# A one-layer HGRN2/gMLP trunk on one core: where the query-key sums, the neighbours' keys, the gate unit's roots and the second group's squares stand in the order of their engines

## Chip, cores and metric

The kernel runs on one core of a Trainium2 chip. The metric is the device time of one execution in microseconds, lower is better. The engines are PE (matrix products), DVE (vector), ACT (scalar functions), POOL (GpSimd) and SP, which issues nearly all the DMAs. PEld is the loading of weights into PE.

## The reference

One layer works on 2048 tokens of 1024 channels, with a context of 256 tokens ahead of it. Cut to what bears on the change:

```python
h = modulate(rmsnorm(x, norm_mix[l]), sh1, sc1)
p = h @ w_in[l]                                   # one projection for both head groups
# group A, 4 heads: gated linear recurrence in both directions
logf, k = log_sigmoid(f), sigmoid(-f)             # per direction
scores = einsum('bhtk,bhsk,bhtsk->bhts', qc, kc, decay)
o = o_inter + einsum('bhts,bhsv->bhtv', scores, vc)
# group B, 4 heads: gMLP gate over chunks of 128 positions
u, v = gelu(u), layernorm(gelu(v))
z = einsum('hpq,bnqhc->bnphc', w_s, v) + b_s
x = x + g1 * (concat(o_hg, u * z) @ w_out[l])
x = x + g2 * conv_ffn(modulate(rmsnorm(x, norm_ffn[l]), sh2, sc2), ...)
return rmsnorm(x, norm_final)
```

## The kernel before

**Stages.** The tokens are worked on in two halves of 1024. For each half the projection runs bank by bank: a bank is 128 columns of w_in times 512 tokens (or the 256 of the context), and it takes three products for each of the eight blocks of 128 channels, since each fp32 operand is split into a high part that is a rounded float (`xh`, `whi`) and a rest (`xl`, `wlo`). `run_banks` writes these products; between them `slot()` lets background work write its next piece. Then follow the output projection, the up-projection with the convolution, the down-projection and the last norm. The changed lines all belong to the stage with the projection, which ends before 960 us of the span.

**The order of the work.** The code is written in one order, and a planner then sets the order in which each engine gets its instructions: it goes by its own reckoning of when the inputs of an instruction are ready, and takes the one that is written first among those that are. `pin` ties an instruction behind the one that is written just before it on the same engine. It orders only these two: an unpinned instruction that is written later may still be put ahead of both. `manual_schedule` keeps the head of the kernel in written order altogether. Each engine works off its own list in order, so an instruction that waits holds up all that stand behind it.

**x's groups.** `x_start` handles the first 1024 tokens in two groups of four tiles of 128 tokens, `xg` and `xs`. For a group `x_square` (L239, ACT) gives the sums of squares, `rstd` (L126 and L128, POOL) the roots, `x_scale` (L245, DVE) multiplies the tiles by them, and `x_first` transposes them on PE and writes `xh` and `xl` (L250, L252, L253) in four steps of two channel blocks each. The squares of the second group are written between steps of the first, and its scaling behind the fourth of them. The weights of a bank are split by `split_w`: a cast on ACT (`whi`, L133) and a subtraction on DVE (`wlo`, L134).

**A head.** `hg` runs eight times, for four heads in each half. It first adds the keys of both directions (L794, DVE), multiplies by the queries (L795), and splits the product into `kh` (L798, a cast on ACT) and `kl` (L800, DVE), whose column sums PE makes with a matrix of ones: these are the query-key sums, the diagonal of the scores. Two more multiplies give `Q` for both directions (L799 and L801). Then the neighbours' products follow (L815, split in L822 into `knl`), and a loop over the levels B = 1, 2, 4, ... 64: PE makes the scores of a level from row 0 of the keys, and DVE masks them in (L846). Then `level_update` multiplies Q (L514), `level_keys` makes the next level's keys in two rows (multiplies in L591, copies on ACT in L594), and `next_tot` the next totals (L521, pinned already). In `level_keys` the loop writes row 0, then row 1. At B = 1 both multiplies are DVE's, and read the gates themselves (`K<-K,F`); these are the neighbours' keys. At higher levels row 1 is POOL's. The result of row 0 overwrites the tile that L822 reads; row 1 lies beside it in the same tile.

**The gate unit.** `sgu` runs eight times too. `ln` takes means and variances (L704, L705), `rstd` the roots on POOL, DVE normalises (L709), PE mixes the positions, DVE adds the bias (L717), and `both` multiplies by gelu(u) on POOL (L685) and stores the result.

Of the kernel before, what the change touches and what calls it, by code (L numbers as in the profile page):

```python
# [9 lines left out]
F32 = mybir.dt.float32  # L10
# [4 lines left out]
ALU = mybir.AluOpType  # L15
# [34 lines left out]
def view(t, off, dims):  # L50

    return bass.AP(t.tensor, t.offset + off, [list(t.ap[0])] + [list(d) for d in dims])
# [32 lines left out]
def tile_trunk(ctx, tc, x, c, cx, c_ctx, w_ada, b_ada, norm_mix, norm_ffn, w_in, hg_norm, sgu_g, sgu_b,  # L85
               w_sp, b_sp, w_out, w_up, conv_w, conv_b, w_down, norm_final, masks, out):
    nc = tc.nc
    V, S, G, T = nc.vector, nc.scalar, nc.gpsimd, Tensor(nc.tensor)
    ld = nc.sync.dma_start
    st = nc.sync.dma_start  # L90
    pin = tc.keep_in_program_order
# [14 lines left out]
    mhalf = cst.tile([P, 8], F32, name="mhalf")  # L106
# [16 lines left out]
    def rstd(pool, ss, n, scale, bias=EPS, keep=lambda i: i, out=None):  # L123

        r = pool.tile([P, 8], F32, tag="rs", name="rs")
        keep(G.tensor_scalar(out=r[:, :n], in0=ss, scalar1=scale, scalar2=bias, op0=ALU.mult, op1=ALU.add))  # L126
        r2 = pool.tile([P, 8], F32, tag="rs2", name="rs2") if out is None else out
        G.tensor_tensor(out=r2[:, :n], in0=r[:, :n], in1=mhalf[:, :n], op=ALU.pow)  # L128
        return r2

    def split(hi, lo, raw, eng=None, keep=lambda i: i):
# [59 lines left out]
    with es1:  # L191
        ps = es1.enter_context(tc.tile_pool(name="ps1", bufs=1, space=PSUM, reuse_waits="tile"))
        p1 = es1.enter_context(tc.tile_pool(name="p1", bufs=1, reuse_waits="tile"))
        pm = es1.enter_context(tc.tile_pool(name="pm", bufs=1, reuse_waits="tile"))
# [38 lines left out]
        def x_sums():  # L233
            return pm.tile([P, 8], F32, tag="xss", name="xss", bufs=2)

        def x_square(xs, ss, i0=0, keep=pin):
            for i, xt in enumerate(xs):
                jk = pm.tile([P, D], BF16, tag="acc", name="xjk")
                keep(S.activation(jk, xt, AF.Square, accum_out=ss[:, i0 + i:i0 + i + 1]))  # L239

        def x_scale(xs, ss, keep=pin):

            r = rstd(pm, ss[:, :len(xs)], len(xs), 1.0 / D, keep=keep)
            for i, xt in enumerate(xs):
                keep(V.tensor_scalar(out=xt, in0=xt, scalar1=r[:, i:i + 1], scalar2=None, op0=ALU.mult))  # L245
# [94 lines left out]
        with tc.manual_schedule():  # L340
# [29 lines left out]
            for k in range(NK):  # L370
                for i in range(2):
                    o = (k % 2) * 256 + i * P
# [43 lines left out]
        def x_start():  # L416
            xk = [pk.tile([P, 2, D], F32, tag="K", name="xk", bufs=2, align_bytes=AL) for i in range(2)]
            xs = [xk[i // 2][:, i % 2, :] for i in range(4)]
            ss, ss2 = ss0, x_sums()
            for q in range(2):  # L420
                x_square(xg[2 * q + 1:2 * q + 3], ss, 2 * q + 1)
                for i in range(2 * q, 2 * q + 2):
                    pin(ld(xs[i], x_rows[4 + i]))
                if q:
                    x_scale(xg, ss)
                yield 2.0
            for i, w in enumerate(x_first(0, xg)):
                if i in (1, 2):
                    x_square(xs[2 * i - 2:2 * i], ss2, 2 * i - 2)
                if i == 3:  # L430
                    x_scale(xs, ss2)
                yield w
            done.add("x0a")
            yield 3.0
            yield from x_first(4, xs)
# [139 lines left out]
        def level_keys(K, B, tot, K2=None):  # L575

            W, nb = TH, TH // B
            K2 = K2 if K2 is not None else pk.tile([P, 2, W], F32, tag="K", name="K2", bufs=2, align_bytes=AL)
            if B == P // 2:
                n = W // (2 * B)  # L580
                src = [[2 * B, n], [B, 2], [1, B]]
                t = view(tot, nb + 1, [[2, n], [-(nb + 1), 2], [0, B]])
                V.tensor_mul(view(K2, 0, [[2 * B, n], [W + B, 2], [1, B]]), view(K, 0, src), t)
                S.copy(view(K2, W, [[2 * B, n], [B - W, 2], [1, B]]), view(K, W, src))
                return K2
            n = W // (4 * B)
            for row, (o, step, t0, ts) in enumerate(((0, 3 * B, nb + 1, 1 - nb), (B, B, 0, nb + 3))):
                src = [[4 * B, n], [step, 2], [1, B]]
                e = G if row and B > 1 else V
                keep = pin if B == 1 else lambda i: i  # L590
                e.tensor_mul(view(K2, row * W + o, src), view(K, o, src), view(tot, t0, [[4, n], [ts, 2], [0, B]]))  # L591
                o2, step2 = (B, B) if row == 0 else (0, 3 * B)
                src = [[4 * B, n], [step2, 2], [1, B]]
                keep(S.copy(view(K2, row * W + o2, src), view(K, W + o2, src)))  # L594
            return K2
# [59 lines left out]
        for h in range(NH):  # L655
            F, K, vt = sets[h % 2]
# [21 lines left out]
        def sgu(hh, h):  # L678

            z, u = {}, {}  # L680

            def both(n0):
                if n0 in z and n0 in u:
                    zt = z.pop(n0)
                    G.tensor_mul(zt, zt, u.pop(n0))  # L685
                    st(oT_d[hh][:, 4 + h, n0:n0 + 512], zt)

            def su(n0, n, pj):
                u[n0] = pm.tile([P, 512], F32, tag="gu", name="gu", bufs=2)
                S.activation(u[n0], pj, AF.Gelu)  # L690
                both(n0)

            def sv(n0, n, pj):
                gv = pm.tile([P, 512], F32, tag="vv", name="gv", bufs=2)
                S.activation(gv, pj, AF.Gelu)

                def ln():
                    pt = bank("mi")
                    for i in range(4):
                        T.transpose(pt[:, i * P:(i + 1) * P], gv[:, i * P:(i + 1) * P], ident)  # L700
                    bs = pm.tile([P, 4, 6], F32, tag="bs", name="bs", bufs=2)
                    mv = pm.tile([P, 4, 2], F32, tag="mv", name="mv", bufs=2)
                    for i in range(4):
                        V.bn_stats(out=bs[:, i, :], in_=pt[:, i * P:(i + 1) * P])  # L704
                        V.bn_aggr(out=mv[:, i, :], in_=bs[:, i, :])  # L705
                    r = rstd(pm, mv[:, :, 1], 4, 1.0)
                    nt = pm.tile([P, 512], F32, tag="nt", name="nt", bufs=2)
                    for i in range(4):
                        V.tensor_scalar(out=nt[:, i * P:(i + 1) * P], in0=pt[:, i * P:(i + 1) * P],  # L709
                                        scalar1=mv[:, i, 0:1], scalar2=r[:, i:i + 1], op0=ALU.subtract, op1=ALU.mult)  # L710

                    def mix():
                        pz = bank("mi")
                        for i in range(4):
                            T.matmul(pz[:, i * P:(i + 1) * P], nt[:, i * P:(i + 1) * P], wsT[:, h, :],
                                     start=True, stop=True)
                        V.scalar_tensor_tensor(out=nt.rearrange("p (c q) -> p c q", q=P),  # L717
                                               in0=pz.rearrange("p (c q) -> p c q", q=P), scalar=sgg[:, h:h + 1],
                                               in1=view(rh, h * P, [[0, 4], [1, P]]), op0=ALU.mult, op1=ALU.add)
                        z[n0] = nt  # L720
                        both(n0)
                    hg_q.later(mix, 7.0)
                hg_q.later(ln, 4.6)
            return su, sv

# [65 lines left out]
        def hg(hh, h, F, K, qs, vt, sgt):  # L791
            Q = ph.tile([P, 2, TH], F32, tag="Q", name="Q", align_bytes=AL)
            kd = Q[:, 0, :]
            V.tensor_add(kd, K[:, 0, :], K[:, 1, :])  # L794
            V.tensor_mul(kd, kd, qs)  # L795
            kh = ph.tile([P, TH], F32R, tag="S", name="kh")
            kl = ph.tile([P, TH], F32R, tag="T1", name="kl")
            S.copy(kh, kd)  # L798
            V.tensor_mul(Q[:, 1, :], qs, F[:, 1, :])  # L799
            V.tensor_sub(kl, kd, kh.bitcast(F32))  # L800
            V.tensor_mul(Q[:, 0, :], qs, F[:, 0, :])  # L801
            yield 6.5
            pbs = [bank("sc") for g in range(2)]
# [9 lines left out]
            K2 = pk.tile([P, 2, TH], F32, tag="K", name="K2", bufs=2, align_bytes=AL)  # L813
# [10 lines left out]
            tot = F  # L824
            for l, B in enumerate(LV):
# [5 lines left out]
                for g in range(0, NCH, 4):  # L831
# [3 lines left out]
                    for i in range(4) if B > 1 else ():  # L835
                        off = (g + i) * P
                        o = pb[:, i * P:(i + 1) * P]
                        if B < 4:
                            o = view(pb, i * P, [[B, 2], [2 * B, P // (2 * B)], [1, B]])
# [9 lines left out]
                K, K2 = level_keys(K, B, tot, K2), None  # L849
                tot = next_tot(tot, TH, B)  # L850
# [4 lines left out]
            for d in range(2):  # L855
                for g in range(0, TH, 512):
                    pt = bank("mi")
                    for i in range(4):
                        o = g + i * P
# [29 lines left out]
            for g in range(0, NCH, 4):  # L889
                po = bank("mi")  # L890
                for i in range(4):
                    ch = g + i
                    sl = slice(ch * P, (ch + 1) * P)
                    o = po[:, i * P:(i + 1) * P]
# [265 lines left out]
        i = len(seq) - 4  # L1160
# [130 lines left out]
    with tc.tile_pool(name="po", bufs=1, reuse_waits="tile") as po:  # L1291
# [58 lines left out]
        xs = []  # L1350
        for t, (hh, g) in enumerate(tiles):
# [12 lines left out]
            o = ops.pop(t)  # L1364
# [16 lines left out]
            if g % 2:  # L1381
# [8 lines left out]
                xs = []  # L1390
# [7 lines left out]
    B = [[xah[:, i] if i < NR else None, xal[:, i] if i < NR - 1 else None] for i in range(7)]  # L1398
# [186 lines left out]
    for n, (u, i) in enumerate(prods):  # L1585
# [30 lines left out]
        if n == NP - 8:  # L1616
            ts = [c_tile().rearrange("p a b -> p (a b)").bitcast(F32) for i in range(2)]
# [20 lines left out]
    V = Kept(nc.vector, pin)  # L1638
# [247 lines left out]
```

## Time and profile before

| | us |
|---|---|
| median of 3 runs | 2433.7 (2433.53 to 2437.77) |
| the profiled execution, its own time | 2434.03 |
| its span in the trace | 2432.2 |

The trace is of one execution. A group of instructions is named by the line that issued it, its engine, and the tiles that it writes and reads (`kl<-Q,kh`); where a helper issues, the line is the helper's, so all matmuls have L66. Rows of the timeline give the start in the span, the duration, engine, line, operation, tiles and shapes, and in brackets how long the engine stood idle before it and what ended that wait. A row `PE sc L66 <- DVE kl L800: 1.1, 2, 0.8` in the view of waits says that PE waited for DVE's L800 for 1.1 us in total, in 2 waits, the longest of 0.8 us. In the view of windows PEclk is the clock granted to PE as a share of its full one.

### The profile page before, as it was taken

Reading aid. Unit: us, or ns where it says so; the run is one execution under the profiler, and the core shown is the slowest. Engines: PE = TensorE matmul, PEld = TensorE weight load, DVE = VectorE, ACT = ScalarE, POOL = GpSimd, SP = SyncE. Lnnn points to the kernel's source line nnn. Section 1 sums busy time; section 2 is a strip of 40 time slices with the busy share of each in tenths; the row PEclk is TensorE's granted clock in tenths of the full one; section 3 lists DMA queues with packets and bytes.
Section 4 is the critical chain, followed back from the end, with each engine's and each line's share of the span. In section 5 each row is a group of like instructions: output and inputs, shape, how many; then the busy total and the mean of one; then the engine's idle time right before and its main releaser. Section 6 shows DMA issues by size and latency. Waiting matters only on the chain.

```text
span 2432.2 us, 32291 instructions
## 1 busy us (share of the span) xinstructions
PE 2400.6 (99%) x11711; PEld 1994.5 (82%) x11711; DVE 1658.0 (68%) x2253; ACT 1044.1 (43%) x1802; POOL 865.0 (36%) x787
## 2 busy tenths in 40 slices
PE   8999999999999999999999999999999999999998
PEld 5887888888888888888788888888888888888887
DVE  5757796765786785565596666639766673676876
ACT  3654344434344443454454444434445443332243
POOL 0021110110121122000688778787888870000002
PEclk9999999999999999999999999999999999999999
DMA  8365545463355234678922222563222239834745
GB/s 303 118 201 168 155 141 175 136 221 112 114 195 173 87 105 152 215 215 262 292 85 90 91 81 91 186 230 96 86 94 84 86 108 387 284 118 148 229 152 199
DMA packets 304046, 393.28 MB, mean 162 GB/s; under 512 B 32634, under 2 KB 215682, under 8 KB 300814
## 3 DMA queue, kind: packets, MB, share of 16 engines
q1 hardware_dynamic: 300596, 390.46, 48.6%
q8 instruction: 92, 1.51, 0.3%
q10 hardware_dynamic: 3289, 0.76, 0.1%
q14 instruction: 69, 0.56, 0.1%
HBM read 283.60 MB, written 107.55 MB: 161 GB/s over the span
## 4 chain that ended last, share of the span: by engine, by line
PE 49%; issue 2%; POOL 1%; DMA 1%; DVE 0%; ACT 0%; SPq 0%; POOLq 0%; ACTq 0%; DVEq 0%
PE ux L66 19%; PE dn L66 16%; PE uz L66 14%; DMA raw<-in_w_up_dram 1%; POOL rr L1746 0%; DMA yf<-yd 0%; POOL Al L134 0%; DMA xn<-cv 0%; POOL ra L1745 0%; POOL ra L1743 0%; DVE fl L134 0%; PE ux L70 0%; ACT jk L1734 0%; ACT yst L133 0%; POOL raw L1260 0%
## 5 line engine op out<-in xcount | busy, mean ns | idle before, releaser
L1451 DVE SCALAR_TENSOR_TENSOR dn<-gp,taps,dn 128x1024 f32<-128x1024 f32 x352 | 447.9, 1283 | 97.4 <-ACT dn L1448 93.0
L66 PE MATMUL dn<-thl,mhl 128*128 128x512 f32 x1680 | 381.0, 389 | 0.0
L66 PEld LDWEIGHTS dn<-thl,mhl 128*128 128x128 f32 x1680 | 315.2, 188 | 65.6 <-issue 0.2
L134 POOL TENSOR_TENSOR Al<-raw,Ah 128x512 fp32r<-128x512 f32 x264 | 341.1, 1308 | 69.0 <-ACT Ah L133 41.1
L66 PE MATMUL pj<-xh,whi 128*128 128x512 f32 x896 | 362.4, 405 | 0.3 <-ACT whi L133 0.3
L66 PE MATMUL pj<-xh,wlo 128*128 128x512 f32 x896 | 351.0, 392 | 0.8 <-DVE wlo L134 0.8
L66 PE MATMUL pj<-xl,whi 128*128 128x512 f32 x896 | 351.7, 392 | 0.0
L133 ACT CAST Ah<-raw 128x512 fp32r<-128x512 f32 x264 | 163.0, 620 | 243.9 <-PE ux L66 125.6
L66 PE MATMUL ux<-xah,Ah 128*128 128x512 f32 x528 | 205.9, 390 | 0.5 <-ACT keep L1515 0.3
L66 PEld LDWEIGHTS pj<-xh,wlo 128*128 128x128 f32 x896 | 168.3, 188 | 36.8 <-DVE wlo L134 1.2
L66 PEld LDWEIGHTS pj<-xh,whi 128*128 128x128 f32 x896 | 168.6, 188 | 34.3 <-issue 3.5
L66 PEld LDWEIGHTS pj<-xl,whi 128*128 128x128 f32 x896 | 168.9, 189 | 30.0 <-DVE xl L253 0.2
L66 PE MATMUL dn<-wo,o 128*128 128x512 f32 x768 | 182.4, 394 | 0.0
L66 PE MATMUL uz<-yf,Ah 128*128 128x512 f32 x704 | 174.0, 389 | 0.0
L591 POOL TENSOR_TENSOR K<-K,tot 128x512 f32<-128x512 f32 x40 | 60.5, 1513 | 300.7 <-DVE tot L521 107.8
L66 PEld LDWEIGHTS dn<-wo,o 128*128 128x128 f32 x768 | 142.1, 188 | 29.1
L66 PE MATMUL ux<-yf,Ah 128*128 128x512 f32 x528 | 155.4, 389 | 0.0
L66 PEld LDWEIGHTS uz<-yf,Ah 128*128 128x128 f32 x704 | 132.1, 188 | 27.4
L66 PE MATMUL ux<-xah,Al 128*128 128x512 f32 x528 | 141.8, 390 | 1.6 <-POOL Al L134 1.6
L66 PE MATMUL ux<-xal,Ah 128*128 128x512 f32 x352 | 137.0, 389 | 0.0
L134 DVE TENSOR_TENSOR wlo<-raw,whi 128x1024 fp32r<-128x1024 f32 x68 | 84.6, 1244 | 71.3 <-ACT whi L133 68.8
L1743 POOL TENSOR_SCALAR ra<-ss 128x1 f32<-128x1 f32 x8 | 3.2, 396 | 359.5 <-ACT jk L1734 359.5
(342 smaller groups left out, 4454.3 us busy)
## 6 DMA issues: line engine op xcount, KB each, us to landing
raw<-in_w_up_dram SPq DMA_DIRECT2D x88, 512.0 KB, 3.6
mr<-m SPq DMA_DIRECT2D x85, 512.0 KB, 5.7
raw<-in_w_in_dram SPq DMA_DIRECT2D x68, 512.0 KB, 4.0
sT<-wd SPq DMA_DIRECT2D x88, 256.0 KB, 5.0
raw<-in_w_ada_dram SPq DMA_DIRECT2D x32, 512.0 KB, 4.3
yf<-yd SPq DMA_DIRECT2D x14, 1024.0 KB, 9.9
m<-cv SPq DMA_DIRECT2D x22, 544.0 KB, 2.7
raw<-in_w_down_dram SPq DMA_DIRECT2D x22, 512.0 KB, 3.7
```

Source lines behind the costliest of these rows:

```text
L66: return self.engine.matmul(out, lhsT, rhs, **kw)
L133: keep(S.copy(hi, raw))
L134: (eng or G).tensor_sub(lo, raw, hi.bitcast(F32))
L591: e.tensor_mul(view(K2, row * W + o, src), view(K, o, src), view(tot, t0, [[4, n], [ts, 2], [0, B]]))
L1451: V.scalar_tensor_tensor(out=cr, in0=gt[:, t // 3:t // 3 + RH, t % 3:t % 3 + GW], scalar=taps[:, t * NF + f:t * NF + f + 1], in1=cr, op0=A ...
L1743: G.tensor_scalar(out=a, in0=ss, scalar1=plus, scalar2=None, op0=ALU.add)
```

## The change

Five things are done. Nothing is added to or taken from what is computed.

- The root in `rstd` (L128) goes through `keep`, as the sum ahead of it (L126) does already, and the gate unit passes `pin` for it.
- The squares of x's second group are written one step of `x_first` later: behind the third and the fourth step in place of the second and the third. Its scaling stays behind the fourth.
- In `level_keys` both multiplies at B = 1 are pinned (at higher levels `keep` does nothing).
- The gate unit's last product on POOL (L685) is pinned.
- In `hg` the add, the multiply by the queries and the subtraction of `kl` are pinned (L794, L795, L800).

```diff
@@ -125,7 +125,7 @@
         r = pool.tile([P, 8], F32, tag="rs", name="rs")
         keep(G.tensor_scalar(out=r[:, :n], in0=ss, scalar1=scale, scalar2=bias, op0=ALU.mult, op1=ALU.add))
         r2 = pool.tile([P, 8], F32, tag="rs2", name="rs2") if out is None else out
-        G.tensor_tensor(out=r2[:, :n], in0=r[:, :n], in1=mhalf[:, :n], op=ALU.pow)
+        keep(G.tensor_tensor(out=r2[:, :n], in0=r[:, :n], in1=mhalf[:, :n], op=ALU.pow))
         return r2
@@ -425,8 +425,8 @@
             for i, w in enumerate(x_first(0, xg)):
-                if i in (1, 2):
-                    x_square(xs[2 * i - 2:2 * i], ss2, 2 * i - 2)
+                if i in (2, 3):
+                    x_square(xs[2 * i - 4:2 * i - 2], ss2, 2 * i - 4)
                 if i == 3:
                     x_scale(xs, ss2)
                 yield w
@@ -588,7 +588,7 @@
                 e = G if row and B > 1 else V
                 keep = pin if B == 1 else lambda i: i
-                e.tensor_mul(view(K2, row * W + o, src), view(K, o, src), view(tot, t0, [[4, n], [ts, 2], [0, B]]))
+                keep(e.tensor_mul(view(K2, row * W + o, src), view(K, o, src), view(tot, t0, [[4, n], [ts, 2], [0, B]])))
@@ -682,7 +682,7 @@
                     zt = z.pop(n0)
-                    G.tensor_mul(zt, zt, u.pop(n0))
+                    pin(G.tensor_mul(zt, zt, u.pop(n0)))
                     st(oT_d[hh][:, 4 + h, n0:n0 + 512], zt)
@@ -703,7 +703,7 @@
-                    r = rstd(pm, mv[:, :, 1], 4, 1.0)
+                    r = rstd(pm, mv[:, :, 1], 4, 1.0, keep=pin)
@@ -791,13 +791,13 @@
             kd = Q[:, 0, :]
-            V.tensor_add(kd, K[:, 0, :], K[:, 1, :])
-            V.tensor_mul(kd, kd, qs)
+            pin(V.tensor_add(kd, K[:, 0, :], K[:, 1, :]))
+            pin(V.tensor_mul(kd, kd, qs))
             kh = ph.tile([P, TH], F32R, tag="S", name="kh")
             kl = ph.tile([P, TH], F32R, tag="T1", name="kl")
             S.copy(kh, kd)
             V.tensor_mul(Q[:, 1, :], qs, F[:, 1, :])
-            V.tensor_sub(kl, kd, kh.bitcast(F32))
+            pin(V.tensor_sub(kl, kd, kh.bitcast(F32)))
             V.tensor_mul(Q[:, 0, :], qs, F[:, 0, :])
```

## Prediction

> **What bounds the kernel now.** First the page, then the waits of PE alone, then the order of time around the places that the change touches.
>
> ```profile
> span 2432.2 us, 32291 instructions
> PE 2400.6 (99%) x11711; PEld 1994.5 (82%) x11711; DVE 1658.0 (68%) x2253; ACT 1044.1 (43%) x1802; POOL 865.0 (36%) x787
> ```
>
> PE sets the time: it is idle for 2432.2 - 2400.6 = 31.6 us of the span. The edits add and remove no instruction, they only reorder DVE, ACT and POOL. They can therefore gain no more than the part of those 31.6 us that these engines cause near the edits, and lose only by new waits of PE. The waits of PE name that part (us in total, times, longest):
>
> ```profile
> PE sc L66 <- DVE K L591: 2.4, 4, 0.9
> PE sc L66 <- DVE Q L514: 1.9, 3, 0.9
> PE pj L66 <- DVE wlo L134: 1.5, 2, 0.8
> PE sc L66 <- DVE kl L800: 1.1, 2, 0.8
> PE pj L66 <- ACT whi L133: 1.1, 2, 0.8
> ```
>
> The first, second and fourth belong to the scores of a head (2.4 + 1.9 + 1.1 = 5.4 us); the other two are weight splits, of which one pair lies beside the moved squares. A measurement of this kernel can tell about 0.2% from no change, which is 4.9 us: nearly all of the 5.4 would have to go before the change counts as faster.
>
> A gap can cost more than itself. These windows are 3.41 us each; after the times stand PE, PEld, DVE, ACT and POOL busy, then the granted clock:
>
> ```profile
> 51.47:54.88 3.41, 2.16 (x17) 1.77 (x16) 2.23 (x5) 1.32 (x2) 0.51 (x1) 1.00 0.67 229
> 54.88:58.29 3.41, 3.21 (x15) 2.63 (x15) 3.41 (x5) 0.63 (x2) 0.00 (x0) 0.50 0.06 14
> 68.53:71.94 3.41, 2.32 (x12) 1.50 (x11) 3.41 (x6) 3.41 (x7) 1.21 (x2) 1.00 0.00 0
> 71.94:75.36 3.42, 3.42 (x23) 2.89 (x22) 3.42 (x7) 2.19 (x5) 0.43 (x1) 1.00 0.55 153
> ```
>
> A window with PE busy for 2.16 us was followed by one at half clock, a window with 2.32 us by one at full clock. A window at half clock loses up to 3.41 / 2 = 1.7 us. The Trainium skill ("TensorE: Matmul & The Clock Gate", Part 1: The HAM clock gate) has the half clock come after at least one idle window of about 3.4 us; by that rule the two charges of 1.7 us in the slower rival below would be nothing, and that rival would end at 2436.0. The trace disagrees: PE was busy for 2.16 of the 3.41 us.
>
> **The change part by part.** I number the eight runs of hg in order of time.
>
> Neighbours' keys (L591 at B = 1). Two DVE multiplies, row 0 and row 1. Row 0 overwrites the tile that L822 still reads, so the one that stands ahead of L822 is row 1. In the fifth head:
>
> ```profile
> 591.00 1.22 DVE L794 TENSOR_TENSOR Q<-K 128x1024 f32<-128x1024 f32 x1
> 592.13 1.14 DVE L591 TENSOR_TENSOR K<-K,F 128x512 f32<-128x512 f32 x1
> 593.19 1.22 DVE L795 TENSOR_TENSOR Q<-Q,qs 128x1024 f32<-128x1024 f32 x1
> 595.52 1.23 DVE L800 TENSOR_TENSOR kl<-Q,kh 128x1024 fp32r<-128x1024 f32 x1 [1.11 <-ACT kh L798]
> ```
>
> ```profile
> 596.80 0.50 PE L66 MATMUL sc<-kl,ones_r 128*128 128x512 f32 x1 [0.76 <-DVE kl L800]
> 413.37 0.50 PE L66 MATMUL sc<-kl,ones_r 128*128 128x512 f32 x1 [0.33 <-DVE kl L800]
> ```
>
> Row 1 sits inside the chain add, multiply, cast, subtract, and delays it by 593.19 - 592.13 = 1.06 us. Pinned, it goes behind row 0, kl comes 1.06 us earlier, and the 0.76 us of the fifth head goes. The third head has the same order, but there a multiply that waits for a load stands ahead of kl:
>
> ```profile
> 411.49 0.69 DVE L993 TENSOR_TENSOR raw<-raw,g 128x512 f32<-128x512 f32 x1 [0.73 <-DMA raw<-in_w_out_dram]
> ```
>
> If it stays there, kl gains nothing. So the gain is 0.76 to 0.76 + 0.33 = 1.09; I take 0.9, since either place of L993 is open.
>
> The other side of this move: L521 is already pinned and is written behind row 1, so the next totals, Q's update and the next keys come later by one such multiply unless the DVE time freed earlier is still in hand. In the last head it isn't, because DVE waits for others in between:
>
> ```profile
> 864.12 1.12 DVE L591 TENSOR_TENSOR K<-K,F 128x512 f32<-128x512 f32 x1
> ...
> 884.85 1.36 DVE L709 TENSOR_SCALAR nt<-mi,mv,rs 128x128 f32<-128x128 f32 x4 [0.86 <-POOL rs L128]
> ...
> 887.26 1.11 DVE L591 TENSOR_TENSOR K<-K,F 128x512 f32<-128x512 f32 x1
> 888.30 1.22 DVE L521 TENSOR_TENSOR tot<-F 128x1024 f32<-128x1024 f32 x1
> ...
> 891.36 2.18 DVE L514 TENSOR_TENSOR Q<-Q,tot 128x1024 f32<-128x1024 f32 x1
> 893.47 0.68 DVE L591 TENSOR_TENSOR K<-K,tot 128x512 f32<-128x512 f32 x1
> ```
>
> ```profile
> 894.29 2.02 PE L66 MATMUL sc<-Q,K 128*128 128x128 f32 x16 [0.73 <-DVE K L591]
> ```
>
> Row 1 leaves 864.12, the wait at 884.85 swallows that, and row 1 comes back at 888.30. PE's wait of 0.73 us at 894.29 grows by up to 888.30 - 887.26 = 1.04 us. What may take it back is that L514 ran beside a multiply on POOL:
>
> ```profile
> 891.17 1.29 POOL L685 TENSOR_TENSOR nt<-nt,gu 128x512 f32<-128x512 f32 x1
> ```
>
> ```profile
> L514 DVE TENSOR_TENSOR Q<-Q,tot x48: 1199/1218/2184, 241.1 to 925.8; 128x1024 f32<-128x1024 f32 x48
> ```
>
> The median L514 takes 1.22 us. Started at 891.36 + 1.04 = 892.40, with POOL done at 892.46, it could end at 893.6 instead of 893.5. The price is thus 0.1 to 1.04; I take 0.6, since POOL's multiply may be late by as much. The Trainium skill ("SBUF — State Buffer", Who interferes with whom) says that a DVE instruction with two inputs in SBUF and a GpSimd instruction that reads SBUF exclude each other for a whole instruction; by it alone the price is 0.1 where POOL keeps its time and 1.04 where it doesn't, and the 2.18 us agree with such a block. The remaining heads I take at nothing: DVE works without a break there between the old and the new place, or PE doesn't wait; the upper bound for each is the 1.04 of the last head.
>
> Query-key sums (L794, L795, L800). A pin puts L794 behind whatever stands ahead of it in written order. In the second head that is a weight split, and it stands behind L794 now:
>
> ```profile
> 314.81 1.22 DVE L794 TENSOR_TENSOR Q<-K 128x1024 f32<-128x1024 f32 x1
> ...
> 317.74 1.22 DVE L134 TENSOR_TENSOR wlo<-raw,whi 128x1024 fp32r<-128x1024 f32 x1
> ...
> 319.54 1.22 DVE L800 TENSOR_TENSOR kl<-Q,kh 128x1024 fp32r<-128x1024 f32 x1
> ```
>
> ```profile
> 316.33 1.05 ACT L133 CAST whi<-raw 128x1024 fp32r<-128x1024 f32 x1 [1.76 <-DMA raw<-in_w_in_dram]
> ```
>
> ```profile
> 320.98 0.40 PE L66 MATMUL sc<-kl,ones_r 128*128 128x512 f32 x1
> ```
>
> This is the wait that the change adds: the split can't start before 316.33 + 1.05 = 317.38, and L794, L795, the cast, kl and all that follows on DVE stand behind it. The split, the add and the multiply issue 1.14 us apart (591.00 to 592.13), so the multiply ends at 317.38 + 2 x 1.14 + 1.22 = 320.9; the cast takes another 1.05 and kl 1.22, so kl ends at 323.2 where PE used it at 320.98: up to 2.2 us late. Nothing is lost if products of the next weights are put ahead of the sums on PE. So 0 to 2.2; I take 0.6, nearer to nothing because PE has such products in every bank.
>
> Roots and the gate's product (L128, L126, L685) on POOL. The root stands directly behind its sum already (see POOL's row below at the squares), and L685 only feeds a store. Nothing; POOL is busy for 36% of the span, which is the cover. Without it a root of the gate unit would be late by one such product, 1.3 us (891.17).
>
> Squares of x's second group. The four squares move one step later; the first two go where the last two are now:
>
> ```profile
> 67.32 1.10 ACT L239 ACTIVATE xjk<-xk 128x1024 bf16<-128x1024 f32 x1
> ...
> 68.36 1.08 ACT L133 CAST whi<-raw 128x1024 fp32r<-128x1024 f32 x1
> 69.30 1.10 ACT L239 ACTIVATE xjk<-xk 128x1024 bf16<-128x1024 f32 x1
> ```
>
> ```profile
> 71.00 0.50 PE L66 MATMUL pj<-xh,wlo 128*128 128x512 f32 x1 [0.77 <-DVE wlo L134]
> ```
>
> ```profile
> 71.08 1.29 POOL L128 TENSOR_TENSOR rs<-rs,mhalf 128x4 f32<-128x4 f32 x1
> ```
>
> The cast of the first x weights sits between two squares and PE waits for its split; that stays, with ACT free some 2 us earlier. At best the 0.77 us goes, at worst both squares come ahead of the cast and it is late by the rest of one. The second group's scaling (no load moves with the squares) comes some two squares later, 2.2 us:
>
> ```profile
> 73.45 2.74 DVE L245 TENSOR_SCALAR xk<-xk,rs 128x1024 f32<-128x1024 f32 x4
> ...
> 90.65 1.36 DVE L253 TENSOR_TENSOR xl<-xfl,xh 128x512 fp32r<-128x512 f32 x2
> ```
>
> PE works on the first group and on context banks meanwhile. So -0.8 to +2.2; I take 0.
>
> **Sum.** -0.9 + 0.6 + 0.6 + 0 = +0.3 us on the profiled execution's 2434.03, which is 2434.3; it lies 0.33 above the median of the runs shown, 2433.7, so I predict 2434.0.
>
> **Rivals.**
> *Slower, 0.18.* One mechanism: the add of a head held behind a split that waits for its load, so that PE's window falls under some 2.2 us busy and the next is at half clock. Place: the second head, price 2.2 + 1.7 instead of 0.6; it decides once a wait of over about 1.1 us falls into one window (3.41 - 2.3), and the last head's 0.73 + 1.04 then does the same, 1.04 + 1.7 instead of 0.6. 2434.0 + 3.3 + 2.1 = 2439.4. For it: the cast there waited 1.76 us for its load. Against it: PE has other products, and 2.2 us late is the far bound.
> *Faster, 0.16.* With the chain straight, every wait of PE for DVE in the scores shrinks: 5.4 us, and 0.77 at the squares. 2433.7 - 6.2 = 2427.5. For it: DVE is at 68%, so order and not load makes these waits. Against it: L514's and L591's waits lie at levels behind row 1's new place.
> *The pins change nothing that PE feels, 0.16.* The seven multiplies move inside stretches in which DVE has no break: 2433.7.
>
> **How the numbers follow.** The forecast has 0.50, and with the last rival the case within 0.2% has 0.66; faster 0.16, slower 0.18. The range takes in the bounds: low 2433.7 - 1.1 - 0.8 - 2.4 (all of L591's waits) = 2429.4, high the slower rival's 2439.4. The forecast's own range is 2432 to 2436.5.
>
> **What would show it.** Right: in every head the two L591 on K<-K,F stand one behind the other; the kl row is gone from PE's waits; the wait at the last head's second level is longer. In the second head the split stands ahead of L794 and PE has a wait near its sums or other products ahead of them. Wrong: more than three windows at half clock, PE's idle time off 31.6 us by more than 5 either way, or a load on SP's queue that comes later because the planner moved it.

## The result and the profile after

| | before | after |
|---|---|---|
| median of 20 runs, us | 2434.57 (2428.89 to 2437.77) | 2438.56 (2434.94 to 2440.56) |
| ratio, 95% interval | | 1.0015 (1.0008 to 1.0022) |
| the profiled execution, its own time | 2434.03 | 2438.55 |

The change costs 4.0 us. The interval leaves no change out; by the bound of 0.2% it is still the case "within 0.2%". The page of after:

```profile
span 2436.7 us, 32286 instructions
PE 2401.0 (99%) x11711; PEld 1993.4 (82%) x11711; DVE 1657.8 (68%) x2253; ACT 1044.5 (43%) x1802; POOL 868.0 (36%) x787
```

PE is idle for 35.7 us where it was 31.6, which is 4.1 of the 4.5 us by which this execution's span is longer: the time went into waits of PE, as it had to, since no instruction was added. The view of PE's waits (total, times, longest) says which:

```profile
PE sc L66 <- DVE K L591: 2.9, 4, 1.1
PE sc L66 <- DVE Q L514: 2.6, 5, 0.9
PE sc L66 <- DVE kl L800: 2.6, 2, 2.1
...
PE mi L70 <- ACT vv L600: 2.0, 1, 2.0
...
PE sc L66 <- ACT kh L798: 0.7, 2, 0.5
...
PE mi L66 <- DVE nt L709: 0.6, 1, 0.6
```

`kl`, which was to go from this list, has grown from 1.1 to 2.6 us; a wait for `vv` is new. Both lie in the third head. In its timeline, first `kl`, then `vv`:

```profile
409.39 1.22 DVE L794 TENSOR_TENSOR Q<-K 128x1024 f32<-128x1024 f32 x1
410.64 1.23 DVE L795 TENSOR_TENSOR Q<-Q,qs 128x1024 f32<-128x1024 f32 x1
414.40 0.69 DVE L993 TENSOR_TENSOR raw<-raw,g 128x512 f32<-128x512 f32 x1 [2.53 <-DMA raw<-in_w_out_dram]
415.01 1.22 DVE L800 TENSOR_TENSOR kl<-Q,kh 128x1024 fp32r<-128x1024 f32 x1
```

```profile
416.28 0.50 PE L66 MATMUL sc<-kl,ones_r 128*128 128x512 f32 x1 [2.06 <-DVE kl L800]
...
439.36 0.92 PE L70 MATMUL mi<-ident,vv 128*128 128x128 f32 x4 [2.03 <-ACT vv L600]
```

```profile
432.89 0.33 SPq L991 DMA_DIRECT2D raw<-in_w_out_dram  x1
```

```profile
436.54 0.69 DVE L993 TENSOR_TENSOR raw<-raw,g 128x512 f32<-128x512 f32 x1 [1.13 <-DMA raw<-in_w_out_dram]
```

```profile
437.26 0.62 ACT L133 CAST raw<-raw 128x512 fp32r<-128x512 f32 x1 [4.20 <-DVE raw L993]
437.78 1.04 ACT L133 CAST whi<-raw 128x1024 fp32r<-128x1024 f32 x1
438.73 0.58 ACT L600 COPY vv<-pj 128x512 f32<-128x512 f32 x1
```

Read the first fence from its brackets. L794 to L795 is the chain without row 1, as the pins wanted it. But w_out's multiply L993 still stands ahead of `kl` and waits 2.53 us for its load, so `kl` starts 4.4 us behind L795. The later fences are the same fault on another engine: L993 waits 1.13 us for the load of 432.89, ACT stands idle for 4.20 us behind L993, and `vv`, which has nothing to do with w_out, stands third in ACT's list. The load itself is hardly slower than before: from its issue to the start of L993 3.65 us pass, and 3.51 us in before (from 429.91 to 433.42). What differs is the order. Before, ACT's order there was `whi`, `vv`, and then w_out's cast:

```profile
431.69 1.04 ACT L133 CAST whi<-raw 128x1024 fp32r<-128x1024 f32 x1 [2.59 <-PE pj L66]
432.64 0.58 ACT L600 COPY vv<-pj 128x512 f32<-128x512 f32 x1
434.14 0.62 ACT L133 CAST raw<-raw 128x512 fp32r<-128x512 f32 x1 [0.92 <-DVE raw L993]
```

The windows of after around both waits (PE, PEld, DVE, ACT, POOL busy, then the granted clock):

```profile
412.30:415.72 3.42, 1.92 (x9) 1.25 (x7) 1.32 (x2) 1.15 (x2) 0.00 (x0) 1.00 0.75 230
415.72:419.13 3.41, 2.85 (x13) 2.38 (x14) 3.38 (x4) 1.08 (x2) 0.00 (x0) 1.00 0.41 135
436.19:439.61 3.42, 1.39 (x10) 0.92 (x9) 2.32 (x3) 2.35 (x4) 1.37 (x1) 1.00 0.01 2
439.61:443.02 3.41, 3.41 (x11) 2.78 (x10) 3.41 (x6) 1.29 (x3) 0.00 (x0) 0.50 0.93 295
```

The two waits are equally long. That for `kl` falls into two windows (PE busy for 1.92 and 2.85 us) and costs itself alone. That for `vv` falls into one, PE is busy for 1.39 us of it, and the next 3.41 us run at half clock: up to 1.7 us on top.

### The profile page after: what moved, and what is told of

Same layout as the page of the kernel before. It is cut to its first block, busy times and chain, and to the rows that moved or that the text cites. A ratio compares the mean times of both kernels' runs of the same rounds, so it can differ in the third digit from the quotient of the medians.

```text
span 2436.7 us, 32286 instructions
## 1 busy us (share of the span) xinstructions
PE 2401.0 (99%) x11711; PEld 1993.4 (82%) x11711; DVE 1657.8 (68%) x2253; ACT 1044.5 (43%) x1802; POOL 868.0 (36%) x787
## 4 chain that ended last, share of the span: by engine, by line
PE 47%; issue 2%; POOL 1%; ACT 0%; DVE 0%; DMA 0%; POOLq 0%; SPq 0%; ACTq 0%
PE ux L66 19%; PE dn L66 14%; PE uz L66 14%; POOL rr L1746 0%; DMA raw<-in_w_up_dram 0%; POOL Al L134 0%; POOL ra L1745 0%; POOL ra L1743 0%; ACT jk L1734 0%; POOL raw L1260 0%; DVE odd L81 0%; DVE dn L1451 0%; POOL raw L1258 0%; POOL fl L1256 0%; POOL s L1256 0%
## 5 line engine op out<-in xcount | busy, mean ns | idle before, releaser
L591 POOL TENSOR_TENSOR K<-K,tot 128x512 f32<-128x512 f32 x40 | 63.3, 1582 | 304.5 <-DVE tot L521 108.4
```

Source lines behind the costliest of these rows:

```text
L591: keep(e.tensor_mul(view(K2, row * W + o, src), view(K, o, src), view(tot, t0, [[4, n], [ts, 2], [0, B]])))
```

## The experiments

The theory after the traces: the pins lengthen no chain by themselves. They make the planner set a new order, in which an operation that waits for w_out's loads stands ahead of `vv` (ACT), as one stood ahead of `kl` (DVE) already. Which edit does so was open.

**Each edit alone**, on before. The four diffs are the hunks of the change.

> Only L794, L795 and L800 are pinned. If the loss comes from the sums (second head held behind the split, then everything behind it late): PE's wait for kh of about 0.5 us in the second head is there, a wait of about 2 us for kl stands in the third head, a window at half clock follows near 440, PE idle is 34 to 36 us and the time about 2438 against 2434.5. If the loss comes from the keys or the squares: PE idle is 31 to 33 us, the third head's wait for kl stays at 0.3 to 0.8, and the time is 2434 to 2435.

> Only L591 at B = 1 is pinned. If the sums are the cause: the fifth head's 0.76 us for kl is gone, the last head's second level waits 1.0 to 1.1 us in place of 0.73, PE idle is 31 to 32 us and the time 2434 to 2435. If the keys are the cause (row 1 behind row 0 puts the loads and splits of w_out later): a wait of about 2 us for kl in the third head, PE idle 34 to 36 us, about 2438.

> Only the squares move. Either theory of the heads: the waits for the split near 70 us (0.32 and 0.77) go and one of about 1 us for the scaled rows near 76 us comes, PE idle 31 to 32 us, 2434 to 2435. If instead the early shift alone sets the order of the loads for all heads: waits of about 2 us near 415 and 439, PE idle 34 to 36 us, about 2438.

> Only the roots and the gate's product on POOL are pinned. Every theory so far: nothing that PE feels, PE idle 31 to 32 us, 2434 to 2435, within 0.1% of before. If it is off by over 0.1% either way, the planner put something else elsewhere because of a pin.

| | median of 11, us | ratio, 95% interval | third head's wait for kl, us |
|---|---|---|---|
| sums | 2436.05 | 1.0007 (0.9998 to 1.0016) | 2.00 |
| keys | 2438.42 | 1.0019 (1.0010 to 1.0028) | 2.08 |
| squares | 2435.53 | 1.0004 (0.9995 to 1.0013) | 2.18 |
| POOL | 2433.31 | 0.9997 (0.9989 to 1.0006) | 0.49 |

before ran beside them at 2434.31. I had suspected the sums, and was wrong: only the keys are resolved, and they alone cost as much as the whole change. The four differences from before (+1.7, +4.1, +1.2 and -1.0 us) add up to 6.0, not to 4.0, but only the second can be told from no change. The keys' trace has the wait for `vv` too (1.37 us), but its window at half clock (from 417.00 us) stands behind the wait for `kl`. The third head's wait for `kl` tells nothing of the edits: it is there at full size with the squares alone, with a window at half clock behind it (from 416.38 us), though from the second head on that kernel's instructions stand in the order of before on every engine. And POOL, which I had put at nothing, takes a wait away. In before, and then with the POOL pins alone:

```profile
921.10 1.00 POOL L126 TENSOR_SCALAR rs<-mv 128x4 f32<-128x4 f32 x1 [5.75 <-DVE mv L705]
922.18 1.29 POOL L685 TENSOR_TENSOR nt<-nt,gu 128x512 f32<-128x512 f32 x1
923.43 1.01 POOL L128 TENSOR_TENSOR rs<-rs,mhalf 128x4 f32<-128x4 f32 x1
...
924.93 1.33 PE L66 MATMUL mi<-wsT,nt 128*128 128x128 f32 x7 [0.86 <-DVE nt L709]
```

```profile
920.54 1.00 POOL L126 TENSOR_SCALAR rs<-mv 128x4 f32<-128x4 f32 x1 [5.77 <-DVE mv L705]
921.62 1.01 POOL L128 TENSOR_TENSOR rs<-rs,mhalf 128x4 f32<-128x4 f32 x1
922.60 1.29 POOL L685 TENSOR_TENSOR nt<-nt,gu 128x512 f32<-128x512 f32 x1
```

The product L685 stood between a sum and its root; now it stands behind both, and PE's wait of 0.86 us is gone. It is gone in all six traces with the POOL pins (the row of `nt L709` above is 0.6 where it was 1.5), and there in all eight without them.

**before once more, the keys in half of the heads, the keys left out, w_out held.** The second kernel pins L591 where `hh == 0`, the third is after without that pin, the fourth is

```diff
-                    V.tensor_mul(w, w, g)
+                    pin(V.tensor_mul(w, w, g))
...
-                        split(hi.bitcast(F32R), w.bitcast(F32R), w, V)
+                        split(hi.bitcast(F32R), w.bitcast(F32R), w, V, pin)
```

> The kernel before once more, for a second execution's trace. If the 2 us that PE waits for kl in the third head (2.08, 2.00 and 2.18 in the runs with the keys, the sums or the squares alone, 0.33 in the first trace of before) are scatter of the w_out loads between executions: between 0.3 and 2.2 here, with the loads L991 near 399 and 409 us off by some us. If they come from what each edit moves: 0.3 to 0.5, and PE idle is 31 to 33 us.

> before, with the keys pinned in the first four heads alone. If the keys cost by what they put ahead of vv on ACT in the fourth head (the w_out cast that waits for a load): PE's wait for vv of 1.4 to 2 us and the window at half clock near 440 are there, the seventh head (near 790 us) has no wait, and the time is 2437 to 2438. If they cost in the seventh and the last head (kh 0.47, kl 0.53, 1.09 in place of 0.73): no more than 2435.

> after without the keys' pin. If the keys bring the wait for vv: it is gone with the window at half clock, and so are the seventh head's 0.16 and 0.53; the fifth head's 0.76 is back; 2434.5 to 2436. If the sums and the squares do as much: 2437 to 2439.

> after, with w_out's multiply and cast (L993, L133) held in written order, behind kl and vv. If they, waiting for their loads, cause the loss: the waits of 2.06 us for kl and 2.03 us for vv and the window at half clock near 440 are gone, PE idle is 31 to 33 us, and the time 2433 to 2435. If the loss is general lateness of DVE in the heads: the waits turn up at other products of the scores, and it stays at 2437 to 2439.

before ran beside these at 2434.09 us.

- before once more, a single execution of 2433.55 us: the wait for `kl` is 1.19 us where the first trace had 0.33. So this wait scatters between executions of one kernel.
- Keys in the first half: 2437.57 us, 1.0015 (1.0006 to 1.0024). Most of the loss lies there. But not as expected: the wait for `kl` is 2.32 us, with the half-clock window behind it, and `vv` makes no wait though ACT has w_out's cast ahead of it. PE, delayed by the first, comes to the products of `vv` as they become ready. The two waits stand in for each other.
- after without the keys: 2434.85 us, 1.0004 (0.9995 to 1.0013). The wait for `vv` is gone, and so are those of the seventh head; the fifth head's 0.76 us is back. `kl` in the third head waits 2.01 us even so, with a window at half clock behind it (from 415.34 us).
- after with w_out held: 2443.99 us (median of 5), 1.0047 (1.0033 to 1.0061), 10 us slower than before. Both waits and the half clock at 440 are gone, as the theory says. But w_out's chain of load, multiply, cast and store ends later, and the second half's x, whose loads stand behind it on SP, arrives late:

```profile
514.60 0.47 PE L66 MATMUL pj<-xh,whi 128*128 128x512 f32 x1 [0.96 <-DMA xh<-xh_d]
515.84 0.50 PE L66 MATMUL pj<-xl,whi 128*128 128x512 f32 x1 [0.77 <-DMA xl<-xl_d]
...
526.60 0.51 PE L66 MATMUL pj<-xh,whi 128*128 128x512 f32 x1 [1.62 <-ACT whi L133]
```

The expectation named no such cost, neither side of it.

**The keys in single heads, and one multiply held.** The first three pin L591 at B = 1 in one head only (the fifth with the POOL pins); the last is

```diff
-                    V.tensor_mul(w, w, g)
+                    (pin if (n, k) == (0, 5) else lambda i: i)(V.tensor_mul(w, w, g))
```

> before, with the keys pinned in the third head alone. Up to 408 us nothing differs from before. If row 1's new place puts w_out's cast ahead of vv on ACT and this alone costs: PE's wait for kl stays at 0.3 to 1.2 us and a wait of 1.4 to 2 us for vv stands near 438; 2435.5 to 2437. If vv is late only because the loads were late already: a wait under 0.5 us there and 2434 to 2435.

> before, with the keys pinned in the second head alone. If the keys cost by making the levels of the second head, and with them the weight sums of w_ada and the loads of w_out, later than PE's products: a wait of 2 us for kl in the third head with a half-clock window behind it, 2436.5 to 2438. If the loss arises in the third head: the wait for kl is 0.3 to 1.2 us and the time 2434 to 2435.

> before with the pins on POOL, and the keys pinned in the fifth head alone. If the prediction's first term holds there: the 0.76 us for kl near 597 is gone and nothing else differs from the run with the pins on POOL alone; PE idle about 0.8 us less than its 30.5, 2432 to 2434. If the pinned row comes back at the next levels: a new wait of up to 1.04 us for Q or K between 600 and 625, and no gain.

> after, with one multiply of w_out (n = 0, k = 5, the one ahead of kl in the third head) held in written order. If this multiply, waiting for its load, makes kl late: the 2.06 us are gone and with the later chain the 2.03 us for vv too; 2434 to 2436 if the chain still ends in time, PE idle 31 to 33. If the chain's later end delays the loads of the second half's x again (waits for xh, xl and whi between 514 and 527, as with all of w_out held): 2438 to 2444.

before ran at 2434.27 us.

*Third head:* 2435.76 us, 1.0006 (0.9997 to 1.0015). The time isn't resolved, the trace is clear. Nothing differs from before up to 408 us, and then:

```profile
414.24 0.50 PE L66 MATMUL sc<-kl,ones_r 128*128 128x512 f32 x1 [1.55 <-DVE kl L800]
...
437.48 0.66 PE L70 MATMUL mi<-ident,vv 128*128 128x128 f32 x4 [2.18 <-ACT vv L600]
```

`vv` waits as in after, with the half clock behind it, with this one pin. The order on ACT is the pin's doing: ACT's list is that of before up to this place, where w_out's cast gets ahead of `whi` and `vv`. That row 1, moved behind row 0, shifts the planner's reckoning by one multiply is how I explain it; no run shows the reckoning. The size of the wait then depends on when the load arrives.

*Second head:* 2436.81 us, 1.0009 (1.0000 to 1.0018). Here PE has new waits of 0.26 (Q) and 0.65 us (`gu`) at its later levels, and 1.94 us for `kl` in the third head with the half clock. The rise is as expected of a chain made late.

*Fifth head, with POOL:* 2433.73 us, 0.9995 (0.9987 to 1.0004). The wait of 0.76 us for `kl` is gone, but a new one stands at the level B = 4:

```profile
618.66 2.02 PE L66 MATMUL sc<-Q,K 128*128 128x128 f32 x16 [0.47 <-DVE Q L514]
```

So the second reading was the right one: row 1 came back, and the pin there is worth 0.3 us. Part of the new wait is another overlap: Q's update (L514) ahead of it takes 1.97 us beside a multiply on POOL (1.29 us at 616.14); with the POOL pins alone it takes 1.30 us. This is the lowest ratio of all, but neither it nor the POOL pins alone can be told from before.

This run shows the scatter best. Up to the fifth head its instructions stand in the same order on every engine as with the POOL pins alone. Those first (wait for `kl`: 0.49 us), then this:

```profile
396.08 0.37 SPq L998 DMA_DIRECT2D wo_d<-raw  x1
399.06 0.33 SPq L991 DMA_DIRECT2D raw<-in_w_out_dram  x1
...
411.51 0.69 DVE L993 TENSOR_TENSOR raw<-raw,g 128x512 f32<-128x512 f32 x1 [0.89 <-DMA raw<-in_w_out_dram]
```

```profile
397.32 0.37 SPq L998 DMA_DIRECT2D wo_d<-raw  x1
401.34 0.33 SPq L991 DMA_DIRECT2D raw<-in_w_out_dram  x1
...
413.81 0.69 DVE L993 TENSOR_TENSOR raw<-raw,g 128x512 f32<-128x512 f32 x1 [1.54 <-DMA raw<-in_w_out_dram]
...
415.69 0.50 PE L66 MATMUL sc<-kl,ones_r 128*128 128x512 f32 x1 [1.79 <-DVE kl L800]
```

L991 waits for the store ahead of it to give its tile free: 2.98 us in one execution, 4.02 in the other. The store itself was 1.24 us later in the second; together that is the lag of 2.3 us with which L993 comes, one round of load, multiply and store further on, and `kl` behind it.

*One multiply held:* 2435.9 us, 1.0007 (0.9998 to 1.0016), between before and after. The waits for `kl` and `vv` of the third head are gone, and x's loads are in time. A part comes back as a wait of 2.00 us for `nt` (L709) at 468.94, which is 0.5 in after. It shows that the multiply ahead of `kl` makes that wait; that the hold makes after faster isn't shown, since the intervals meet.

## Why the prediction was right, and where not

2434.0 was forecast with 2429.4 to 2439.4 around it, and 2438.56 came: the range and the likeliest case, within 0.2%, hold. The sum does not. It had +0.3 us for the change, and 4.0 were measured; the forecast's own range, 2432 to 2436.5, was missed. That the wide one holds is partly luck: its upper end is the slower rival's, worked out for another place than the one that cost. (Its lower end lies above the 2427.5 us of the faster rival, which it should have taken in.) By the terms of the sum:

- **Keys, the gain (-0.9).** The mechanism was right and the size wrong: the 0.76 us of the fifth head went, but 0.46 us came back in after at 620 (0.47 in the run of that head). It is worth 0.3. The third head's `kl` gained nothing, since L993 stayed ahead of it, as one of the two cases said.
- **Keys, the last head (+0.6).** Right; 0.73 became 1.09, which is +0.36. The reason given for the lower half holds as well: L514 again runs beside POOL's product and takes 2.22 us.

```profile
894.32 2.14 DVE L591 TENSOR_TENSOR K<-K,F 128x512 f32<-128x512 f32 x2
896.38 1.22 DVE L521 TENSOR_TENSOR tot<-F 128x1024 f32<-128x1024 f32 x1
...
899.42 2.22 DVE L514 TENSOR_TENSOR Q<-Q,tot 128x1024 f32<-128x1024 f32 x1
```

```profile
899.26 1.30 POOL L685 TENSOR_TENSOR nt<-nt,gu 128x512 f32<-128x512 f32 x1
```

```profile
902.39 2.02 PE L66 MATMUL sc<-Q,K 128*128 128x128 f32 x16 [1.09 <-DVE K L591]
```

- **"The remaining heads I take at nothing."** This is the step that failed. I asked only whether DVE's own work comes later, and bounded it by one multiply, 1.04 us. What the keys' pin did in the third head was to change ACT's list, so that `vv` waits for a load: 2.03 us in place of before's 0.47 for Q at that level, and up to 1.7 us by the half clock. In the second head it added the levels' waits. In the seventh, new waits for `kh` and `kl` (0.16 and 0.53 us in after) stand in all four traces that pin the keys there, and in no other. The fault is the same there, on DVE and without a load: with row 1 gone from its old place, L737, which waits 2.85 us for a root on POOL, comes ahead of a head's add L794. In before it ran at 788.15, behind L794 at 784.14 and without a wait; the four traces have the new order and the wait, and no other has.

```profile
789.41 0.69 DVE L737 TENSOR_TENSOR on<-on,rk 128x512 f32<-128x512 f32 x1 [2.85 <-POOL rk L128]
```

```profile
796.38 0.73 PE L66 MATMUL sc<-kh,ones_r 128*128 128x512 f32 x2 [0.16 <-ACT kh L798]
797.64 0.74 PE L66 MATMUL sc<-kl,ones_r 128*128 128x512 f32 x2 [0.53 <-DVE kl L800]
```

- **Sums (+0.6 in the second head).** Right. L794 stands behind the split, and PE waits 0.50 us for `kh` (0.43 with the sums alone) where the sums were in time before; four products of the projection, which the planner put between the sums of `kh` and those of `kl`, hide the rest.

```profile
316.10 1.23 DVE L134 TENSOR_TENSOR wlo<-raw,whi 128x1024 fp32r<-128x1024 f32 x1 [1.78 <-ACT whi L133]
317.24 1.22 DVE L794 TENSOR_TENSOR Q<-K 128x1024 f32<-128x1024 f32 x1
...
321.38 0.73 PE L66 MATMUL sc<-kh,ones_r 128*128 128x512 f32 x2 [0.50 <-ACT kh L798]
```

- **Roots and product on POOL (0).** Wrong by -0.86. I took one place in x's stage, where the root stood behind its sum, for all of them. The price that I gave for a root behind the product, 1.3 us, was being paid already, by the gate unit beside the last head, and 0.86 of it reached PE.
- **Squares (0).** Right, as a sum of two: the 0.77 us for `wlo` went with the wait for `whi` ahead of it (0.32), and 1.04 us for the scaled rows came.

```profile
76.23 0.30 PE L70 MATMUL mi<-ident,xk 128*128 128x128 f32 x1 [1.04 <-DVE xk L245]
```

**The rivals.** The slower one had the right kind of mechanism (an operation held behind one that waits for a load, and half a clock behind it) and nearly the right size, 2439.4. Its place was wrong: not the add in the second head, but `vv` on ACT in the third, and not the sums' pin but the keys'. Its point of decision, a window under 2.2 us, was off too: 1.92 left the clock at full. The faster rival fell; no wait of the scores shrank without another growing. The third, that PE feels nothing, fell with the interval, which leaves no change out.

**The signs.** Of those named for a right prediction, the two L591 do stand one behind the other in all eight heads, the last head's wait is longer, and PE waits near the second head's sums; the row of `kl` did not go. Two of the signs named for a wrong one did not show this loss: idle time grew by 4.1 us where 5 was the bound, and after has three windows at half clock ahead of its last microseconds (from 47, 54 and 440 us), as many as before (38, 48 and 55).

**What remains open.** The third head's wait for `kl` was 0.33, 1.19, 0.49, 1.79 and 2.18 us in five traces (before twice, POOL, the fifth head's keys, the squares) whose lists from the second head to this place are one and the same, so 2.06 us in after is within its scatter. In the six that change the second head's order, the two that hold work of w_out aside, it was 1.94 to 2.32 each time. Whether it is longer there on average can't be told from one trace each, and so neither how the 4.0 us divide between this wait and that for `vv`.

For the one pair of traces the division can be read by setting the starts of PE's products in after against those of the same products in before. After falls back by 2.5 us in the second head (300 to 411 us of before), 1.7 at `kl`, 3.2 at `vv` with the half clock, 1.4 in the seventh head and 0.3 in the last. It gains 1.2 us by the POOL pins and 3.0 ahead of 300 us and behind 965 us. So `vv` is the largest single place, but only about a third of the 9.1 us that these places lose together. With the keys alone, as slow by its median, `kl` cost 3.3 us and `vv` 0.8: the sizes change from trace to trace. What the runs show is that the keys' pin costs, and in several places at once.

## What to carry to other kernels

- Under a planner, a pin on one engine reorders the others. Ask of every instruction that waits for a transfer or for another engine which unrelated work stands behind it on DVE and ACT: a pin's loss may appear there, on another engine than the pin's.
- A chain made shorter at one level may pay at the next; follow the moved instruction until its engine next stands idle, and count that place too.
- A wait that is scattered between executions of the same program must not be charged to an edit. Run an edit that changes nothing ahead of that place, and look whether the wait moves.

## What was not expected of the hardware

**What halves the clock.** PE's windows before a half-clock window were busy for 1.39 us (after, near 438) and, near 415, for 1.63 us with the keys in the fifth head:

```profile
413.30:416.72 3.42, 1.63 (x6) 1.05 (x6) 2.91 (x4) 0.81 (x3) 0.00 (x0) 1.00 0.67 214
416.72:420.13 3.41, 3.41 (x10) 2.65 (x9) 3.34 (x4) 1.96 (x4) 0.00 (x0) 0.51 0.27 77
```

1.92 us (after, 412.30) kept it, while 2.16 us in x's stage did not, nor did 2.65 us there with the keys in the second head (from 49.59). So busy time alone doesn't decide. Between 60 and 960 us, over all traces, the border lies between 1.76 us (w_out held, from 523.54; half clock behind it) and 1.82 us (one multiply held, from 465.12; full clock) of 3.41 us. By the Trainium skill ("TensorE: Matmul & The Clock Gate", Part 1: The HAM clock gate) an idle window is needed; here windows that PE filled by 32% (1.09 us, the keys in the first half, from 414.01) to 52% (1.76 us) were enough.

**A store's time.** From the issue of a 512-KB store to the issue of the load that needs its tile, 2.98 and 4.02 us passed in executions of the same list of instructions. With a window at half clock hanging on it, one such microsecond could by estimate cost 2.7 (1 and the 1.7 of the window). This may be a part of why before itself spreads over 2428.89 to 2437.77 us; no run tests it, and neither of the two traces of before has such a window in the heads.
